# Queueing the expert rows of a gather behind the sums on VectorE, and lending it one weight buffer

## The chip, the core and the metric

The kernel is one program on one core of a Trainium2 chip. The metric is device time in microseconds. Three timed runs of the kernel before gave 3833.3, 3834.04 and 3835.98 us; the median is 3834.04 us. One further execution was taken by the profiler, and all rows below are of that one.

## The reference, cut to what matters

The program computes two transformer blocks over 512 tokens of width 1024. All work of this change lies in the last step of the second block, a feed-forward layer that looks up experts:

```python
def peer_ffn(h, peer_w_q, peer_keys_1, peer_keys_2, peer_u, peer_v):
    ht = h.reshape(T, D)                       # T = 512 tokens, D = 1024
    ...                                        # scores, top 16 of 128 x 128 pairs, 8 heads
    experts = (...).reshape(T, 128)            # 128 expert numbers of 16384 per token
    gates = softmax(sc).reshape(T, 128)
    u = peer_u[experts]                        # 128 rows of 1024 per token
    act = gelu(einsum('cd,ced->ce', hc, u))
    return einsum('ce,ced->cd', gates * act, peer_v[experts])

h = layer_norm(ALPHA * h + peer_ffn(h, ...), ln2_g, ln2_b)
```

## The kernel before, in words

The 512 tokens are split. For the last 384 of them the layer is computed densely: TensorE multiplies them by all of `peer_u`, the gelu of the products is multiplied by a matrix of gates that is zero outside the chosen experts, and the result is multiplied by all of `peer_v`. For the first 128 tokens the chosen rows are gathered from HBM, one expert of each of the 128 tokens at a time.

**The dense part.** Weights come as chunks of 128x1024 f32 (512 KB). `Stream` holds four raw buffers. `load` (L148) issues the chunk's DMA from SyncE's queue as soon as a raw buffer is free. `cut` splits a chunk into a high and a low half: ScalarE casts the high half (L155), VectorE subtracts it to get the low half (L157), and then the raw buffer is free again. There are three pairs of split buffers, so that the cut of a chunk waits until the product three before it has read its pair. A product is 24 matmuls (L281, L282, L283; the third reads the low half) of 128x384 into one PSUM bank. There are 128 "u" products (`ups`, first matrix) and 128 "v" products (second matrix, 16 groups `c` of 8). 31 u products are made ahead of the last loop; in the loop each v product from the ninth on is followed by one u product until all 128 are made, and the last 23 v products stand alone. Behind each v product the code lists, in this order: `weigh` (L2005 on VectorE multiplies a gelu by its gates; L287 on ScalarE and L288 on VectorE split it), `settle` of the v product before (L2032 on VectorE adds its PSUM bank to the sum), and `rows`, which is the gather.

**The gather.** It is a generator. `fetch(n)` (L1953) is an indirect DMA on GpSimd's queue that brings 512 KB, one row of 1024 f32 for each of 128 tokens, into one of three row buffers. Rows 0 to 127 come from the first matrix, and L1966 on VectorE multiplies each by the token's state and sums it up to one number; rows 128 to 255 come from the second, and L1968 on VectorE adds each, times its gate, to an accumulator. Before row n is used, the fetch of row n + 2 is issued; it must wait until row n - 1 has been used, whose buffer it takes. After row 255 there is a layer norm of the first 128 tokens (L1974 to L1985) and its store.

`rows(products)` paces the gather in the order of the code: 256 rows over `work` = 128 + 128 - 31 - 8 = 217 products. That is the order in which the code lists the instructions. The order on the engines is made by a planner, which keeps time estimates of its own: an instruction that it takes to be ready is put on its engine ahead of instructions listed earlier. Each engine then runs its own list strictly in order.

Of the kernel before, what the change touches and what calls it, by code (L numbers as in the profile page):

```python
# [10 lines left out]
OP = mybir.AluOpType  # L11
AX = mybir.AxisListType

D = 1024
# [13 lines left out]
ALPHA = 2.0**0.25  # L28
# [7 lines left out]
class Buf:  # L36
    def __init__(self, arena, off, n, ap):
        self.arena, self.off, self.n, self.ap = arena, off, n, ap
# [78 lines left out]
class Stream:  # L117
# [6 lines left out]
    def __init__(self, k, order=None, nraw=4, nsplit=3):  # L124
        self.k, self.order, self.nraw, self.nsplit = k, order, nraw, nsplit
        self.chunks = {}
        self.free = [k.F(1024, top=True) for _ in range(nraw)]
        self.hl = [(k.R(1024, top=True), k.R(1024, top=True)) for _ in range(nsplit)]
        self.rest = k.nc.vector
        self.asked = []  # L130
        self.seen = {}
        self.held = False
        self.loaded = self.split = self.cuts = self.used = 0
        self.whole = None

    def add(self, key, aps):
        c = self.chunks.setdefault(key, [])
# [3 lines left out]
    def load(self, i):  # L141
# [6 lines left out]
        self.k.nc.sync.dma_start(c[1].ap, c[0])  # L148
        return True

    def cut(self, i):
        key, n = self.order[i]
        c = self.chunks[key][n]
        hi, lo = self.hl[self.cuts % self.nsplit]
        self.k.nc.scalar.copy(hi.ap, c[1].ap)  # L155
        eng = self.rest[i % len(self.rest)] if isinstance(self.rest, list) else self.rest
        eng.tensor_tensor(lo.ap, c[1].ap, hi.ap.bitcast(F32), op=OP.subtract)  # L157
        self.free.append(c[1])
        c[1] = hi.ap, lo.ap
        self.cuts += 1  # L160

# [60 lines left out]
class K:  # L222
# [1508 lines left out]
    def peer(self):  # L1731

        nc = self.nc
# [20 lines left out]
        sel0 = self.F(384, top=True)  # L1754
# [65 lines left out]
        def up(j):  # L1820
            for _ in ups(j):
                pass
# [5 lines left out]
        for n in range(16):  # L1828
            if n in first:
                ps = first[n]  # L1830
            else:
                hi, lo = self.ws.get("wq")
                ps = self.bank()
# [54 lines left out]
        for t in (1, 2, 3):  # L1888
            sv3 = st.v(4, 128)
            nxt = None  # L1890
            for g in range(16):
                c = slice(g * 8, g * 8 + 8)
# [12 lines left out]
                if fused:  # L1905
                    for r in range(8):
                        q = slice(g * 8 + r, g * 8 + r + 1)
                        nc.vector.tensor_scalar(e2[:, r * 128 : r * 128 + 128], iota.ap, sv3[:, 1, q], sv3[:, 2, q],  # L1908
                                                op0=OP.is_equal, op1=OP.mult)
                else:  # L1910
                    w = e2.rearrange("p (a b) -> p a b", a=8)
                    nc.gpsimd.tensor_tensor(w, w, sv3[:, 2, c, None].to_broadcast([128, 8, 128]), op=OP.mult)
                stage = stages[g // 2 % len(stages)]
                for half in range(2):
                    ps = self.bank()
                    for q in range(4):
                        r = half * 4 + q
                        w = slice(r * 128, (r + 1) * 128)
# [12 lines left out]
            st.free()  # L1931
            st = nxt
        row.free()
        while ahead < sum(UPS):
            up(ahead)
            ahead += 1
            yield 3.9
# [6 lines left out]
        def gather():  # L1944

            s0 = sel0.v(3, 128)
            ids, act0 = self.F(128), self.F(128)
            acc0 = self.F(D)
            rows = [self.F(D) for _ in range(3)]

            def fetch(n):
                if n < 256:
                    nc.gpsimd.indirect_dma_start(out=rows[n % 3].ap, out_offset=None, in_=self.a["u" if n < 128 else "vv"],  # L1953
                                                 in_offset=bass.IndirectOffsetOnAxis(ap=ids.ap[:, n % 128 : n % 128 + 1].bitcast(U32), axis=0))

            nc.vector.scalar_tensor_tensor(act0.ap, s0[:, 0], 128.0, s0[:, 1], op0=OP.mult, op1=OP.add)
            nc.vector.tensor_copy(ids.ap.bitcast(U32), act0.ap)
            nc.vector.tensor_scalar(acc0.ap, ht.ap, ALPHA, None, op0=OP.mult)
            for n in range(2):
                fetch(n)  # L1960
            yield
            for n in range(256):
                r = rows[n % 3].ap
                fetch(n + 2)
                if n < 128:
                    nc.vector.scalar_tensor_tensor(r, r, 1.0, ht.ap, op0=OP.mult, op1=OP.mult, accum_out=act0.ap[:, n : n + 1])  # L1966
                else:
                    nc.vector.scalar_tensor_tensor(acc0.ap, r, act0.ap[:, n - 128 : n - 127], acc0.ap, op0=OP.mult, op1=OP.add)  # L1968
                if n == 127:
                    nc.scalar.activation(act0.ap, act0.ap, AF.Gelu_apprx_tanh)  # L1970
                    nc.vector.tensor_mul(act0.ap, act0.ap, s0[:, 2])
                yield
            for j in range(2):
                nc.gpsimd.dma_start(rows[j].ap, self.a["ln2"][:, j * D : (j + 1) * D])  # L1974
            w, scr = self.F(8), rows[2].ap
            W = w.ap
            nc.vector.tensor_reduce(W[:, 0:1], acc0.ap, axis=AX.X, op=OP.add)
            nc.vector.tensor_scalar(W[:, 0:1], W[:, 0:1], 1.0 / D, None, op0=OP.mult)
            nc.vector.tensor_scalar(acc0.ap, acc0.ap, W[:, 0:1], None, op0=OP.subtract)
            nc.scalar.activation(scr, acc0.ap, AF.Square, accum_out=W[:, 1:2])  # L1980
            nc.scalar.activation(W[:, 2:3], W[:, 1:2], AF.Sqrt, bias=self.eps6.ap[:, 1:2], scale=1.0 / D)
            nc.vector.reciprocal(W[:, 3:4], W[:, 2:3])
            nc.vector.scalar_tensor_tensor(scr, acc0.ap, W[:, 3:4], rows[0].ap, op0=OP.mult, op1=OP.mult)
            nc.vector.tensor_add(scr, scr, rows[1].ap)
            nc.sync.dma_start(self.out0, scr)  # L1985
            for x in rows + [w, acc0, sel0, ids, act0]:
                x.free()


# [23 lines left out]
        for g in range(2):  # L2013
            ps = self.bank()
# [8 lines left out]
        for k in range(KT):  # L2023
            nc.gpsimd.tensor_tensor(av[:, k].rearrange("p (t n) -> p t n", t=3), hh[:, 1:, k].bitcast(F32),
                                    hl[:, 1:, k].bitcast(F32), op=OP.add)
        gat = gather()
        down = []

        def settle(c, d, seg, ps):
            c0, c1 = seg  # L2030
            x = av[:, d, c0:c1]
            nc.vector.scalar_tensor_tensor(x, x, ALPHA if c == 0 else 1.0, ps.ap[:, : c1 - c0], op0=OP.mult, op1=OP.add)  # L2032
            ps.free()
            if c == 15:
                t = tot[seg]
                if d == 1:
                    nc.vector.tensor_add(t.ap, av[:, 0, c0:c1], x)
                elif 1 < d < 7:
                    nc.vector.tensor_add(t.ap, t.ap, x)

        self.ws.rest = nc.vector
        ws = {}
        work = 128 + 128 - ahead - 8
        paced = [0, 0]

        def rows(products):

            paced[0] += products
            while paced[1] < 256 * paced[0] // work:
                next(gat, None)  # L2050
                paced[1] += 1


# [11 lines left out]
        for c in range(16):  # L2065
            cur = [ws.pop(c * 8 + j) for j in range(8)]
            for seg in last if c == 15 else [(0, N)]:
                c0, c1 = seg
                if c == 15:
                    tot[seg] = self.F(c1 - c0)  # L2070
                for d in range(8):
                    hi, lo = self.ws.get("v_b" if c0 else "v")
                    ps = self.bank()
                    for j in range(8):
                        self.mm3(ps.ap[:, : c1 - c0], hi[:, j * 128 : (j + 1) * 128], lo[:, j * 128 : (j + 1) * 128],
                                 *[w[:, c0:c1] for w in cur[j]], j == 0, j == 7)
                    self.ws.done()
                    n = 1
                    if c and ahead < 128:
                        n = 2  # L2080
                        up(ahead)
                        ahead += 1
                        if ahead == 128:
                            gelu(*late.pop())
                        yield 3.9
                    weigh(c * 8 + 8 + d)
                    down.append((c, d, seg, ps))
                    if len(down) > 1:
                        settle(*down.pop(0))
                    rows(n)  # L2090
                    if not c0 and d in (1, 3, 5):
                        gload(c + 2, d // 2)
                    self.tick()
                    yield 3.9
                if c == 15:
                    settle(*down.pop(0))
                    if seg != last[-1]:
                        self.later(self.last_norm(av, seg, tot[seg]))
# [438 lines left out]
```

## Time and profile before

| what | value |
|---|---|
| median of three timed runs | 3834.04 us |
| profiled execution | 3846.21 us, span of its trace 3844.5 us |
| TensorE (PE) busy | 3598.5 us, 94% of the span |
| VectorE (DVE) busy | 2461.9 us, 64% |
| ScalarE (ACT) busy | 1455.4 us, 38% |
| GpSimd (POOL) busy | 711.4 us, 19% |
| mean granted clock of TensorE | 0.971 of full speed |

PE are matmuls, PEld their weight loads. The loop with the gather is the last part of the span, from about 2782 us; the page's row of 40 slices shows DMA engines busy at 8 and 9 tenths in slices 29 to 37 and at 2 to 4 tenths in most others. A group of the view by lines reads: line, engine, operation, result <- operands, shapes, count | busy us, mean ns of one | idle us of that engine just before them and what ended it. DVE durations overlap their neighbours' a little at the ends.

### The profile page before, as it was taken

To read this page: it belongs to the slowest core of one execution; us is meant where nothing else is said; L and a number is where in the kernel's file an instruction comes from. 1 tells how busy PE (TensorE), PEld (TensorE's weight loads), DVE (VectorE), ACT (ScalarE), POOL (GpSimd) and SP (SyncE) were. 2 spreads that over 40 slices of the span, in tenths; PEclk is the share of its full clock that TensorE was granted. 3 is DMA by queue.
4 is the path that set the end of the run, shared out by engine and by line. 5 is a ranking of instruction groups with operands and counts; after the bars stand their busy time and mean duration, and the time that the engine had idled before them with its cause. 6 is when DMAs were issued, how large, how long until landed. Compare 5 with 4: busy or idle time off the path is not lost. (4 is left out here: it accounts for less than half of the span.)

```text
span 3844.5 us, 51080 instructions
## 1 busy us (share of the span) xinstructions
PE 3598.5 (94%) x20063; PEld 3168.7 (82%) x20063; DVE 2461.9 (64%) x4157; ACT 1455.4 (38%) x2351; POOL 711.4 (19%) x511
## 2 busy tenths in 40 slices
PE   7999899999999999998999898888889999999997
PEld 4766588888888888887888867878789999889997
DVE  6543675343466555657544657898988777777754
ACT  5323444222244333335323546425633333332332
POOL 1111100000000000000000110665534444444200
PEclk9999999999999999998999998999999999999998
DMA  5355432212122212122322312324788888888732
GB/s 204 118 197 187 151 127 85 65 62 65 62 95 89 73 63 86 58 75 72 115 95 97 129 60 95 102 85 143 211 309 313 305 304 308 291 302 298 269 126 72
DMA packets 199597, 573.38 MB, mean 149 GB/s; under 512 B 17051, under 2 KB 67227, under 8 KB 199356
## 3 DMA queue, kind: packets, MB, share of 16 engines
q1 hardware_dynamic: 100224, 362.33, 28.7%
q0 software_dynamic: 42416, 156.57, 11.4%
q10 hardware_dynamic: 56716, 51.22, 4.0%
q8 instruction: 157, 2.57, 0.3%
q14 instruction: 84, 0.69, 0.0%
HBM read 539.64 MB, written 30.41 MB: 148 GB/s over the span
## 5 line engine op out<-in xcount | busy, mean ns | idle before, releaser
L155 ACT CAST ra<-fa 128x1024 fp32r<-128x1024 f32 x591 | 620.1, 1051 | 1591.6 <-PE P L282 655.0
L157 DVE TENSOR_TENSOR ra<-fa,ra 128x1024 fp32r<-128x1024 f32 x543 | 663.0, 1223 | 491.2 <-ACT ra L155 484.2
L282 PE MATMUL P<-ra 128*128 128x512 f32 (+1 forms) x1952 | 694.5, 357 | 2.9 <-DVE ra L288 2.7
L283 PE MATMUL P<-ra 128*128 128x512 f32 (+1 forms) x1872 | 675.3, 363 | 2.4 <-DVE ra L157 2.4
L281 PE MATMUL P<-ra 128*128 128x512 f32 (+1 forms) x1824 | 651.0, 364 | 21.1 <-ACT ra L287 17.4
L283 PE MATMUL bank<-ra 128*128 128x384 f32 (+2 forms) x1648 | 564.4, 343 | 63.1 <-DVE ra L157 41.8
L281 PE MATMUL bank<-ra 128*128 128x384 f32 (+2 forms) x1648 | 561.7, 342 | 13.0 <-ACT ra L287 11.4
L282 PE MATMUL bank<-ra 128*128 128x384 f32 (+2 forms) x1648 | 560.0, 340 | 8.3 <-DVE ra L288 8.3
L281 PE MATMUL P<-mR,ra 128*128 128x512 f32 (+1 forms) x1344 | 464.7, 349 | 12.8 <-ACT mR L287 8.6
L283 PE MATMUL P<-mR,ra 128*128 128x512 f32 (+1 forms) x1344 | 459.2, 343 | 0.3 <-DVE ra L157 0.3
L282 PE MATMUL P<-mR,ra 128*128 128x512 f32 (+1 forms) x1216 | 424.3, 350 | 1.0 <-DVE mR L288 1.0
L282 PEld LDWEIGHTS P<-ra 128*128 128x128 f32 x1952 | 375.4, 192 | 56.1 <-DVE ra L288 3.7
L281 PEld LDWEIGHTS P<-ra 128*128 128x128 f32 x1824 | 346.7, 192 | 78.7 <-ACT ra L287 19.5
L283 PEld LDWEIGHTS P<-ra 128*128 128x128 f32 x1872 | 357.9, 191 | 57.7 <-DVE ra L157 3.7
L283 PEld LDWEIGHTS bank<-ra 128*128 128x128 f32 x1648 | 317.7, 193 | 79.9 <-DVE ra L157 53.2
L281 PEld LDWEIGHTS bank<-ra 128*128 128x128 f32 x1648 | 317.8, 193 | 17.8 <-ACT ra L287 12.0
L282 PEld LDWEIGHTS bank<-ra 128*128 128x128 f32 x1648 | 317.9, 193 | 12.5 <-DVE ra L288 9.3
L876 DVE SCALAR_TENSOR_TENSOR fa<-P,fa 128x512 f32<-128x512 f32 (+1 forms) x256 | 164.1, 641 | 221.8 <-PE P L283 221.4
L281 PEld LDWEIGHTS P<-mR,ra 128*128 128x128 f32 x1344 | 257.5, 193 | 52.7 <-ACT mR L287 10.0
L283 PEld LDWEIGHTS P<-mR,ra 128*128 128x128 f32 x1344 | 256.7, 192 | 31.1 <-DVE ra L157 1.1
L282 PEld LDWEIGHTS P<-mR,ra 128*128 128x128 f32 x1216 | 232.0, 191 | 32.5 <-issue 2.2
L1968 DVE SCALAR_TENSOR_TENSOR fa<-fa 128x1024 f32<-128x1024 f32 x128 | 164.0, 1281 | 87.4 <-DMA fa<-in_vv,fa 86.9
(418 smaller groups left out, 5395.2 us busy)
## 6 DMA issues: line engine op xcount, KB each, us to landing
fa<-in_w SPq DMA_DIRECT2D x144, 512.0 KB, 3.7
fa<-in_ud SPq DMA_DIRECT2D x128, 512.0 KB, 4.8
fa<-in_vd SPq DMA_DIRECT2D x128, 512.0 KB, 5.7
fa<-in_ada SPq DMA_DIRECT2D x96, 512.0 KB, 4.9
fa<-in_od_in SPq DMA_DIRECT2D x66, 512.0 KB, 3.7
gd<-fa ACTq DMA_DIRECT2D x24, 1024.0 KB, 5.3
trio<-gd ACTq DMA_DIRECT2D x48, 512.0 KB, 9.0
fa<-in_w_q SPq DMA_DIRECT2D x22, 512.0 KB, 3.8
```

The costliest lines, as they stand in the source:

```text
L155: self.k.nc.scalar.copy(hi.ap, c[1].ap)
L157: eng.tensor_tensor(lo.ap, c[1].ap, hi.ap.bitcast(F32), op=OP.subtract)
L281: mm(ps, wh, xh, start=start, stop=False)
L282: mm(ps, wh, xl, start=False, stop=False)
L283: mm(ps, wl, xh, start=False, stop=stop)
L876: self.nc.vector.scalar_tensor_tensor(x, ps, g[:, n, kind : kind + 1], x, op0=OP.mult, op1=OP.add)
L1968: nc.vector.scalar_tensor_tensor(acc0.ap, r, act0.ap[:, n - 128 : n - 127], acc0.ap, op0=OP.mult, op1=OP.add)
```

## The change

Each step of the gather is listed with an order edge: its VectorE instructions stand on VectorE's list behind the last `settle` that the code has listed (`issue_after`; it is an order, not a wait for a semaphore). The gather gets a fourth row buffer, and the fetch of row n + 3 is issued before row n is used. The fourth buffer is one of `Stream`'s four raw buffers: the first chunk that is cut after the page stage gives its buffer to the gather (`lend`) instead of back to the stream, which has three from then on.

```diff
@@ class Stream @@
+    def lend(self, f):
+
+        self.lent = f
...
     def cut(self, i):
...
-        self.free.append(c[1])
+        if self.lent:
+            self.lent(c[1])
+            self.lent = None
+        else:
+            self.free.append(c[1])
@@ def peer @@
         row.free()
+        lent = []
+        self.ws.lend(lent.append)
         while ahead < sum(UPS):
             up(ahead)
...
-            rows = [self.F(D) for _ in range(3)]
+            own = [self.F(D) for _ in range(3)]
+            rows = own + lent
 
             def fetch(n):
                 if n < 256:
-                    nc.gpsimd.indirect_dma_start(out=rows[n % 3].ap, ...
+                    nc.gpsimd.indirect_dma_start(out=rows[n % 4].ap, ...
...
-            for n in range(2):
+            for n in range(3):
                 fetch(n)
             yield
             for n in range(256):
-                r = rows[n % 3].ap
-                fetch(n + 2)
+                r = rows[n % 4].ap
+                fetch(n + 3)
...
-            for x in rows + [w, acc0, sel0, ids, act0]:
+            for x in own + [w, acc0, sel0, ids, act0]:
                 x.free()
@@ def settle @@
-            nc.vector.scalar_tensor_tensor(x, x, ALPHA if c == 0 else 1.0, ps.ap[:, : c1 - c0], op0=OP.mult, op1=OP.add)
+            i = nc.vector.scalar_tensor_tensor(x, x, ALPHA if c == 0 else 1.0, ps.ap[:, : c1 - c0], op0=OP.mult, op1=OP.add)
+            settled[:] = [getattr(i, "ins", i)]
...
+        settled = []
@@ def rows @@
             while paced[1] < 256 * paced[0] // work:
-                next(gat, None)
+
+                with self.tc.issue_after(settled[0]) if settled else nullcontext():
+                    next(gat, None)
                 paced[1] += 1
```

## Rows read from the trace of the kernel before

**Rows 1.** Busy time by stretch: stretch, length, engines busy (count), PE clock, DMA share, GB/s
```profile
2782.00:2860.00 78.00, 64.20 (x353) 62.87 (x352) 59.80 (x103) 27.06 (x44) 28.55 (x25) 0.89 0.85 301
2860.00:3620.00 760.00, 717.36 (x4015) 704.36 (x4014) 598.10 (x772) 240.73 (x332) 314.92 (x240) 0.98 0.87 304
3620.00:3817.00 197.00, 197.00 (x1139) 197.00 (x1138) 102.40 (x133) 66.62 (x88) 0.55 (x1) 1.00 0.37 121
```
**Rows 2.** What PE waited for from 2860 to 3620: us in total, times, longest
```profile
PE bank L283 <- DVE ra L157: 41.4, 29, 4.5
```
**Rows 3.** What DVE waited for from 2860 to 3620
```profile
DVE fa L1968 <- DMA fa<-in_vv,fa: 86.9, 55, 4.9
DVE fa L1966 <- DMA fa<-in_u,fa: 74.2, 50, 4.1
```
**Rows 4.** DVE in order of time: start, us, line, operation, idle before and its end
```profile
3342.94 1.29 DVE L1968 SCALAR_TENSOR_TENSOR fa<-fa 128x1024 f32<-128x1024 f32 x1 [1.34 <-DMA fa<-in_vv,fa]
...
3348.77 2.61 DVE L1968 SCALAR_TENSOR_TENSOR fa<-fa 128x1024 f32<-128x1024 f32 x2 [2.95 <-DMA fa<-in_vv,fa]
3351.29 1.22 DVE L157 TENSOR_TENSOR ra<-fa,ra 128x1024 fp32r<-128x1024 f32 x1
```
**Rows 5.** ACT in order of time, the same stretch
```profile
3345.46 1.05 ACT L155 CAST ra<-fa 128x1024 fp32r<-128x1024 f32 x1 [2.32 <-PE bank L282]
```
**Rows 6.** PE in order of time, the same stretch
```profile
3352.57 0.44 PE L283 MATMUL bank<-ra 128*128 128x384 f32 x1 [2.23 <-DVE ra L157]
```
**Rows 7.** The gather's fetches, line L1953, up to 3204 us (durations in ns)
```profile
L1953 POOL DMA_INDIRECT fa<-in_u,fa x127: 932/1016/1878, 2786.5 to 3199.4; - x127
...
DMA to landing us min/median/max: 4.2/6.8/12.6
```
**Rows 8.** The same from 3206 to 3620 us
```profile
L1953 POOL DMA_INDIRECT fa<-in_vv,fa x128: 936/1295/3286, 3206.5 to 3615.1; - x128
...
DMA to landing us min/median/max: 4.2/7.0/11.2
```
**Rows 9.** POOL in order of time: a fetch behind the row that frees its buffer
```profile
3344.49 0.94 POOL L1953 DMA_INDIRECT fa<-in_vv,fa  x1 [2.09 <-DVE fa L1968]
```
**Rows 10.** DVE by lines from 2860 to 3620
```profile
L157 DVE TENSOR_TENSOR ra<-fa,ra 128x1024 fp32r<-128x1024 f32 x168 | 204.2, 1218 | 0.0
L1968 DVE SCALAR_TENSOR_TENSOR fa<-fa 128x1024 f32<-128x1024 f32 x127 | 162.7, 1281 | 87.3 <-DMA fa<-in_vv,fa 86.9
L1966 DVE SCALAR_TENSOR_TENSOR fa<-fa 128x1024 f32<-128x1024 f32 x114 | 139.1, 1221 | 74.6 <-DMA fa<-in_u,fa 74.2
L2005 DVE TENSOR_TENSOR cols<-cols,trio 128x384 f32<-128x384 f32 x84 | 46.2, 550 | 0.0
L2032 DVE SCALAR_TENSOR_TENSOR fa<-fa,bank 128x384 f32<-128x384 f32 x84 | 45.9, 546 | 0.0
L288 DVE TENSOR_TENSOR cols<-cols 128x384 fp32r<-128x384 f32 x45 | 24.8, 550 | 0.0
L288 DVE TENSOR_TENSOR ra<-cols,ra 128x384 fp32r<-128x384 f32 x35 | 17.8, 550 | 0.0
```
**Rows 11.** The weights' loads, line L148, from 2786 to 3620 us
```profile
L148 SPq DMA_DIRECT2D fa<-in_vd x91: 327/328/328, 2788.4 to 3616.5; - x91
...
who waited for it (us, times):
  ACT ra L155: 3.9, 1
...
DMA to landing us min/median/max: 3.6/5.9/13.2
```
**Rows 12.** What SyncE's queue waited for from 2860 to 3620
```profile
SPq L148 <- DVE ra L157: 691.9, 168, 8.8
```
**Rows 13.** DVE in order of time: the last two sums of products
```profile
3813.49 0.55 DVE L2032 SCALAR_TENSOR_TENSOR fa<-fa,bank 128x384 f32<-128x384 f32 x1 [3.01 <-PE bank L283]
...
3817.65 0.56 DVE L2032 SCALAR_TENSOR_TENSOR fa<-fa,bank 128x384 f32<-128x384 f32 x1 [3.02 <-PE bank L283]
```
**Rows 14.** DVE in order of time: the gather's last rows and the end of its layer norm
```profile
3619.72 2.60 DVE L1968 SCALAR_TENSOR_TENSOR fa<-fa 128x1024 f32<-128x1024 f32 x2
...
3630.72 1.22 DVE L1984 TENSOR_TENSOR fa<-fa 128x1024 f32<-128x1024 f32 x1
```
**Rows 15.** What PE waited for from 2780 to 2860
```profile
PE bank L281 <- ACT ra L287: 6.0, 1, 6.0
PE bank L282 <- DVE ra L288: 4.8, 1, 4.8
PE bank L283 <- DVE ra L157: 2.8, 1, 2.8
```

More of the change, by code (lines that the diff above doesn't have):

```diff
@@ L1 @@
 import math
+from contextlib import nullcontext
 import numpy as np
@@ L133, in __init__ @@
         self.loaded = self.split = self.cuts = self.used = 0
-        self.whole = None
+        self.whole = self.lent = None
     def add(self, key, aps):
@@ L1948, in gather @@
             acc0 = self.F(D)
-            rows = [self.F(D) for _ in range(3)]
+            own = [self.F(D) for _ in range(3)]
+            rows = own + lent
             def fetch(n):
                 if n < 256:
-                    nc.gpsimd.indirect_dma_start(out=rows[n % 3].ap, out_offset=None, in_=self.a["u" if n < 128 else "vv"],
+                    nc.gpsimd.indirect_dma_start(out=rows[n % 4].ap, out_offset=None, in_=self.a["u" if n < 128 else "vv"],
                                                  in_offset=bass.IndirectOffsetOnAxis(ap=ids.ap[:, n % 128 : n % 128 + 1].bitcast(U32), axis=0))
```

## The prediction, written before the change was run

> **What bounds the kernel now.** I read the busy times by stretch first. From 3620 us on, when the gather is over, TensorE never stops: 1139 matmuls in 197.0 us at full granted clock, 173.0 ns each [rows 1]. The last two sums, one product apart, start 4.16 us apart [rows 13]: 24 matmuls of 173.3 ns. That is the cadence of this loop when nothing is late. From 2860 to 3620 us, beside the gather, 4015 matmuls take 760 us [rows 1]; at the cadence they would take 4015 x 0.1733 = 695.8 us. So 64 us are lost beside the gather, and this is all that a change to the gather can win here.
>
> The view of waits says who takes them. TensorE waits 41.4 us in 29 waits, practically all of its idle time there, for the low half of a weight chunk, which VectorE cuts [rows 2]. The other 23 us go with the clock: it was granted at 0.98 on the mean in this stretch against 1.00 behind it [rows 1]. Mean 0.98 of the levels 1.2 and 2.4 GHz is 4% of the time at the low one, 30 us, half of which is lost; the rest is the restart after each wait.
>
> VectorE is busy 598 of the 760 us [rows 1], so it isn't full. Its idle time is 161 us, all of it spent at the head of a gather row whose DMA had not landed, in 105 of 241 rows [rows 3, 10]. Three rows in order of time show how this reaches TensorE. ScalarE's half of a cut starts at 3345.46 [rows 5] and ends 1.05 us later. VectorE's half could follow; but two gather rows stand ahead of it, the first of them waits 2.95 us for its DMA, and the cut starts at 3351.29 [rows 4], 4.8 us after its input. TensorE waits 2.23 us for it [rows 6].
>
> **Why the rows are late.** With three row buffers, a fetch starts when the row three before has been used: the row at 3342.94 ends at 3344.23 and its buffer's fetch starts at 3344.49, 0.26 us later [rows 4, 9]. It lands 6.8 to 7.0 us after its start on the median, 12.6 at most [rows 7, 8]. So a buffer turns round in 0.3 + 6.9 + 1.3 (the row itself [rows 10]) = 8.5 us, and three buffers give at best a row per 2.8 us. The rows were planned faster than the DMAs could bring them: 241 rows for 84 sums of products [rows 10], 2.87 per v product. The code lists 2 x 256 / 217 = 2.36 per v product with its u product.
>
> **The change, part by part.**
>
> *The edge.* A v and a u product last 8.32 us at the cadence. With the edge no more than 2.36 rows on the mean stand behind each sum, so a row is wanted every 3.53 us.
>
> *The fourth buffer.* Four buffers of 8.5 us give a row per 2.1 us at best, well ahead of 3.53. But rows now come in bursts of 2 or 3 behind each sum, back to back. Row n is fetched when row n - 4 ends. At 2.36 on the mean, 36% of the bursts have three rows. Most rows have two bursts of lead, over 14 us, more than any landing. The tight ones are: the second row of a burst of two behind a burst of three (fetched behind the first row of the burst before; 8.3 us), and the third row of a burst of three behind a burst of two (8.32 + 1.2 = 9.5 us). Each occurs in about 36% of 97 pairs. A landing is 0.3 + 6.9 = 7.2 us after the buffer is free on the median, and from 4.5 to 12.9. I estimate that a third of the first kind and a sixth of the second come late, by 1.2 us: 97 x 0.36 x 0.5 x 1.2 = 21 us of VectorE waiting instead of 161. In this trace 161 us of it cost TensorE 64 us, 0.40 each; so 8 us stay lost. Bounds: 0 if no row is late enough to matter (a cut has slack, below), 32 us if half of the waiting stays.
>
> The Trainium skill, "DMA: Bandwidth & Descriptors", section "Anatomy of one DMA", gives a DMA from GpSimd's queue as about 2.0 us plus its bytes at 436 GB/s: an estimate of 3.2 us for 512 KB. The trace shows 6.8 to 7.0 beside the weights' loads, and by 3.2 us three buffers would never have been late, which they were 105 times; the measurement decides. By the page, the 8 us would be 0 and the time 8 us less.
>
> *VectorE's load.* Per pair: two cuts of 1.22, one sum, one `weigh` and one split of 0.55 each, and 2.36 rows of 1.25 us are 7.04 us nominal [rows 10]. The lines of the view add up to 650 us of which 598 are distinct (ends overlap [rows 1, 10]), so 6.5 of 8.32 us, 78%. The worst queue ahead of a cut is a sum and three rows, 0.5 + 3 x 1.2 = 4.1 us from the end of a product; the cut's input is ready 1.2 us after the same moment, so the low half is ready 5.3 us after it and is wanted two products later, at 8.3. 3 us of slack: this hides the burst, and a row that is late by less.
>
> In the last 23 v products, which stand alone, the gather still has 256 - 2 x 97 x 256 / 217 - 9 = 18 rows, over 15 products. There VectorE has 1.22 + 3 x 0.55 + 1.18 x 1.28 = 4.38 nominal, 4.03 distinct, per 4.16 us. This phase runs without loss today because the gather is over [rows 1]. Cost 0 at 4.03, 15 x (4.38 - 4.16) = 3 us at the nominal price; I take 3, since waits for ScalarE come on top.
>
> *The gather's end.* Its layer norm takes 11 to 12 us behind the last row [rows 14]. It is listed behind product 218 of 225, so with 29 us of products still to come, and the other tokens' norm of 27 us behind these [rows 1]: hidden. If the rows fell 15 us behind, it would start to compete with the last norm.
>
> *Three raw buffers.* Each load is issued at the end of a cut, 168 times of 168 [rows 12]. The cut of product i waits for the end of product i - 3; it then takes 1.05 on ScalarE, a delay d until VectorE comes to it, and 1.22. The load behind it, now for product i + 3, lands 5.9 us later (13.2 at most [rows 11]); it is wanted 3 products = 12.48 us after the cut could start. So 8.2 + d against 12.48 us: d may be 4.3 us. In the forecast d is 0 to 3 us. If a chunk is late, its own cut may still slip by 6 - d us before TensorE waits. Four buffers never ran dry (one wait of 3.9 us, at the start [rows 11]). I take 0; the other end is the last rival.
>
> *The start.* From 2782 to 2860 us TensorE loses some 22 us, half of it waiting for the first weighted columns [rows 1, 15], which the change doesn't touch; 2.8 us wait for a cut [rows 15]. I take 0, between 3 us lost (a third fetch ahead of the first loads) and 5 won.
>
> **The sum.** 64 - 8 - 3 = 53 us. The profiled execution took 3846.2 us, 1.7 over its span; it becomes 3793. The median of the timed runs lies 12.2 us under the profiled one, so 3834 - 53 = 3781 us.
>
> **The rivals.**
>
> *Rows still late.* Two or three fetches now start within 4 us of each other, and GpSimd writes them one by one, 1.0 to 1.3 us each and up to 3.3 [rows 7, 8]. If the landing of a burst's last fetches grows by 2 us, the 8.3 us kind is late as a rule and the 9.5 us kind half the time: 97 x 0.36 x (1.5 + 0.8) = 80 us of VectorE waiting, 32 us of TensorE's. Gain 64 - 32 - 3 = 29: 3805 us. For it: the spread from 4.2 to 12.6 us. Against it: the pace falls from 2.87 to 2.36 rows per pair, and with it the load on the DMA engines of 0.87. A rule of the Trainium skill would make it so: by "SBUF — State Buffer", section "Who interferes with whom", a VectorE instruction with two SBUF inputs keeps a GpSimd instruction that reads SBUF waiting, and a burst is several such instructions end to end. The long fetch of 3.3 us would fit that; the medians near 1.0 and 1.3 us, beside a VectorE that was busy 79% of the stretch, speak against a regular cost.
>
> *It doesn't do what it says.* The edge keeps rows from running ahead, but whether a cut stands behind them is still the planner's choice. If VectorE waits for rows as long as now, or idles at the head of a sum for the product's end and is as late with cuts, the 64 us stay: 3834 us. Against it: 8.5 us of turn-round against 4 x 3.53.
>
> *Three raw buffers starve TensorE.* This decides for slower, in one place: the loop load, cast, cut, load. A late chunk costs TensorE, per pair, (2.3 + d + landing) - 12.48 - (6 - d) = landing + 2d - 16.2 us. With the 4.8 us of delay seen at 3351 in every v product's cut and landings of 7.5 us, it is 0.9 us x 97 = 87 us lost against 64 won: 3857 us. It starts to cost at landings of 6.6 us with that d, at 10.2 with d = 3, and to outweigh the gain 0.7 us above either. Landings reach 13.2 us [rows 11], but the median is 5.9, and d of 4.8 came from a DMA wait that the change shortens.
>
> **How the numbers follow.** Forecast 3781 us, chance 0.62, with its own range of 3764 (all 64 us and some of the start) to 3797 (16 us more lost). Rows still late, 3797 to 3822: 0.20. Nothing won, about 3834: 0.08. Starved, from 3842 up: 0.10. Two tenths lie outside 3762 to 3812, nearly all above. A difference under 0.2%, 7.7 us, can't be told from none here. Faster takes the first two, 0.82.
>
> **What would show it.** Right: in the loop, VectorE's waits for rows fall from 161 to about 20 us and TensorE's for L157 from 41 to under 10; the granted clock is 0.99 or 1.00; sums come 8.3 us apart beside u products; the last row is used some 30 us before the last product's end, not 200. Wrong: VectorE's wait for rows stays above 80 us; ScalarE's casts wait for the weights' DMA; TensorE waits in the last 23 products; or the end waits for the gather's norm.

## The result, and the profile after

The changed kernel took 3779.07 us (median of four runs, 3772.22 to 3780.1) against 3835.01 for the kernel before (its three runs and a fourth of 3843.63): a ratio of 0.9842 (95% interval 0.983 to 0.9855). Forecast were 3781 us. Its profiled execution took 3780.1 us, its trace spans 3778.4.

Busy time by stretch, the changed kernel (stretch, length, then PE, PEld, DVE, ACT, POOL busy with counts, PE clock, DMA share, GB/s):

```profile
2782.00:2860.00 78.00, 67.19 (x378) 65.62 (x377) 60.19 (x104) 29.16 (x45) 31.28 (x25) 0.91 0.85 289
2860.00:3620.00 760.00, 757.61 (x4372) 757.29 (x4371) 600.74 (x784) 261.39 (x360) 310.28 (x216) 1.00 0.85 300
3620.00:3751.00 131.00, 131.00 (x757) 131.00 (x756) 100.04 (x120) 42.93 (x57) 37.31 (x26) 1.00 0.63 214
```

Beside the gather, the same 760 us now hold 4372 matmuls instead of 4015 [rows 1]. At 173.3 ns each they account for 757.7 us, so 2 us are lost where 64 were. The granted clock is 1.00. The last 131 us, with the v products that stand alone and the end of the gather among them, lose nothing. What TensorE and VectorE wait for from 2860 to 3620 us, the changed kernel (settle is L2044 now, the gather's rows L1978 and L1980, a chunk's cast and low half L160 and L162):

```profile
PE bank L292 <- DVE ra L162: 2.4, 1, 2.4
```
```profile
DVE fa L2044 <- PE bank L292: 93.2, 82, 1.6
DVE ra L162 <- ACT ra L160: 57.6, 54, 1.4
DVE fa L1978 <- DMA fa<-in_u,fa: 7.4, 4, 3.2
DVE fa L1980 <- DMA fa<-in_vv,fa: 0.4, 1, 0.4
```

TensorE's 29 waits for a low half [rows 2] have become one. VectorE's idle time has changed its owner: before it stood at rows that had not landed [rows 3]; now it stands at the head of a sum whose product TensorE hasn't finished, or of a low half whose cast ScalarE hasn't made. VectorE now waits for TensorE, 82 times of the 92 sums. VectorE's list in order of time:

```profile
3302.28 0.56 DVE L2044 SCALAR_TENSOR_TENSOR fa<-fa,bank 128x384 f32<-128x384 f32 x1 [1.31 <-PE bank L292]
3302.75 1.28 DVE L1980 SCALAR_TENSOR_TENSOR fa<-fa 128x1024 f32<-128x1024 f32 x1
3303.95 1.22 DVE L162 TENSOR_TENSOR ra<-fa,ra 128x1024 fp32r<-128x1024 f32 x1
3305.09 1.28 DVE L1980 SCALAR_TENSOR_TENSOR fa<-fa 128x1024 f32<-128x1024 f32 x1
3307.35 1.23 DVE L162 TENSOR_TENSOR ra<-fa,ra 128x1024 fp32r<-128x1024 f32 x1 [0.99 <-ACT ra L160]
3308.49 0.55 DVE L2017 TENSOR_TENSOR cols<-cols,trio 128x384 f32<-128x384 f32 x1
3308.96 0.55 DVE L297 TENSOR_TENSOR cols<-cols 128x384 fp32r<-128x384 f32 x1
3310.60 0.56 DVE L2044 SCALAR_TENSOR_TENSOR fa<-fa,bank 128x384 f32<-128x384 f32 x1 [1.09 <-PE bank L292]
```

Two sums start 8.32 us apart: two products at the cadence. Here, with rows of the second matrix, they are not in a block behind the sum; the planner has set a low half between them, 0.8 us after its cast (ScalarE's cast of this chunk starts at 3302.11 and takes 1.05 us). With rows of the first matrix they are: from 2860 to 3620 us three of them stand end to end behind a sum 16 times and two 29 times. One of the 16 (the lines of the accumulator's read left out):

```profile
2944.52 0.56 DVE L2044 SCALAR_TENSOR_TENSOR fa<-fa,bank 128x384 f32<-128x384 f32 x1 [1.09 <-PE bank L292]
2944.99 1.22 DVE L1978 SCALAR_TENSOR_TENSOR fa<-fa 128x1024 f32<-128x1024 f32 x1
...
2946.14 1.22 DVE L1978 SCALAR_TENSOR_TENSOR fa<-fa 128x1024 f32<-128x1024 f32 x1
...
2947.28 1.22 DVE L1978 SCALAR_TENSOR_TENSOR fa<-fa 128x1024 f32<-128x1024 f32 x1
...
2948.43 2.39 DVE L162 TENSOR_TENSOR ra<-fa,ra 128x1024 fp32r<-128x1024 f32 x2
```

The gather's DMAs land no sooner than before:

```profile
DMA to landing us min/median/max: 4.8/7.7/13.5
```

But they are issued so much earlier that a row lies landed for 4.4 us on the median before VectorE takes it, instead of 0.15 us before (each fetch of the stretch matched with its row in the two traces).

### The profile page after: what moved, and what is told of

The parts are those of the page before. It is cut to its first block, busy times and chain, and to the rows that moved or that the text cites. A ratio compares the mean times of both kernels' runs of the same rounds, so it can differ in the third digit from the quotient of the medians.

```text
span 3778.4 us, 51080 instructions
## 1 busy us (share of the span) xinstructions
PE 3578.4 (95%) x20063; PEld 3161.0 (84%) x20063; DVE 2463.2 (65%) x4157; ACT 1452.7 (38%) x2349; POOL 746.2 (20%) x511
## 5 line engine op out<-in xcount | busy, mean ns | idle before, releaser
L160 ACT CAST ra<-fa 128x1024 fp32r<-128x1024 f32 x591 | 620.2, 1051 | 1534.2 <-PE P L291 653.9
L162 DVE TENSOR_TENSOR ra<-fa,ra 128x1024 fp32r<-128x1024 f32 x543 | 663.2, 1224 | 508.2 <-ACT ra L160 501.3
L292 PE MATMUL bank<-ra 128*128 128x384 f32 (+2 forms) x1648 | 555.1, 338 | 21.0 <-POOL ra L162 21.0
L290 PE MATMUL bank<-ra 128*128 128x384 f32 (+2 forms) x1648 | 556.4, 339 | 13.3 <-ACT ra L296 12.0
L291 PE MATMUL bank<-ra 128*128 128x384 f32 (+2 forms) x1648 | 555.1, 337 | 7.1 <-DVE ra L297 7.1
L292 PEld LDWEIGHTS bank<-ra 128*128 128x128 f32 x1648 | 313.9, 191 | 26.8 <-POOL ra L162 23.4
L290 PEld LDWEIGHTS bank<-ra 128*128 128x128 f32 x1648 | 314.0, 191 | 17.9 <-ACT ra L296 12.6
L291 PEld LDWEIGHTS bank<-ra 128*128 128x128 f32 x1648 | 314.2, 191 | 11.3 <-DVE ra L297 8.1
L1965 POOL DMA_INDIRECT fa<-in_vv,fa x128 | 189.3, 1479 | 265.9 <-DVE fa L1980 251.6
```

The lines of the kernel that those rows point to most:

```text
L290: mm(ps, wh, xh, start=start, stop=False)
L291: mm(ps, wh, xl, start=False, stop=False)
L292: mm(ps, wl, xh, start=False, stop=stop)
L1965: nc.gpsimd.indirect_dma_start(out=rows[n % 4].ap, out_offset=None, in_=self.a["u" if n < 128 else "vv"], in_offset=bass.IndirectOffsetOnA ...
```

## Experiments

All were timed against the kernel before. The third column is 760 us less 0.1733 us for each matmul in the stretch from 2860 to 3620 us, from each run's own busy times, as for the 64 us of before [rows 1]; the fourth is what VectorE waited there for rows' DMAs; then rows per v product with its u product, counted on VectorE.

| kernel | ratio (95% interval) | TensorE loses, us | VectorE waits for rows, us | rows per pair |
|---|---|---|---|---|
| before (three buffers) | 1 | 64 | 161 | 241 / 84 = 2.87 |
| the change | 0.9842 (0.983 to 0.9855) | 2 | 8 | 216 / 92 = 2.35 |
| edge alone (three) | 0.9833 (0.982 to 0.9847) | 5 | 73 | 217 / 91 = 2.38 |
| edge alone, again | 0.9851 (0.9836 to 0.9866) | 0 | 64 | 218 / 92 = 2.37 |
| buffer alone (four) | 0.9856 (0.9841 to 0.9871) | 3 | 42 | 195 / 66 = 2.95 |
| edge, three, pace 2.75 | 0.9968 (0.9958 to 0.9978) | 44 | 153 | 239 / 86 = 2.78 |
| edge, three, pace 3.0 | 0.9984 (0.9972 to 0.9996) | 58 | 152 | 242 / 85 = 2.85 |
| edge, four, pace 3.0 | 0.9858 (0.9842 to 0.9873) | 4 | 30 | 192 / 65 = 2.95 |
| no fetches | 0.9825 (0.9811 to 0.9838) | 0 | 0 | 223 / 65 = 3.4 |

(For the buffer alone, for four buffers at pace 3.0 and for the kernel without fetches, the rows per pair are of 2860 to 3400 us, as their gathers end within the longer stretch. In the last of them rows are no DMAs, but VectorE's instructions.)

**The edge alone.** The change without `lend`, three row buffers, the fetch two rows ahead.

```diff
-        self.ws.lend(lent.append)
...
-            rows = own + lent
+            rows = own
...
-            for n in range(3):
+            for n in range(2):
                 fetch(n)
...
-                r = rows[n % 4].ap
-                fetch(n + 3)
+                r = rows[n % 3].ap
+                fetch(n + 2)
```

> The order edge alone: three row buffers, the fetch two rows ahead, four raw weight buffers. My theory: edge and buffer are both needed. A row is wanted every 3.53 us and three buffers of 8.5 us can bring one per 2.8, so on the mean they keep up; but the lead of a row is 3 x 3.53 - 1.25 = 9.3 us (less where rows stand together) against landings of 7.2 us on the median and up to 12.9, so a good part of the rows is late: VectorE waits 50 to 100 us for rows instead of 161, TensorE's loss is 20 to 40 us of 64, the time 0.989 to 0.995 of before. Rival A, the pace is the whole gain: VectorE waits under 20 us, the time is that of the full change, 0.984 to 0.986. Rival B, the buffer is the whole gain: VectorE waits 130 us or more and the time is within 0.3% of before.

It came out as fast as the full change. VectorE waits 73 us for rows, as my theory had it; TensorE loses 5 us, not 20 to 40. Its waits from 2860 to 3620 us, TensorE's and VectorE's (L1977 and L1979 are the rows here):

```profile
PE bank L292 <- DVE ra L162: 3.7, 4, 1.7
```
```profile
DVE fa L2043 <- PE bank L292: 58.1, 59, 1.6
DVE fa L1977 <- DMA fa<-in_u,fa: 57.6, 38, 5.2
DVE ra L162 <- ACT ra L160: 25.7, 28, 1.3
DVE fa L1979 <- DMA fa<-in_vv,fa: 14.9, 15, 2.2
```

In 53 waits, one of 5.2 us, a late row holds VectorE up, and TensorE hardly notices. So "late rows cost TensorE 0.40 us each microsecond" is false, and so is "edge and buffer are both needed".

**The fourth buffer alone.** The change without `issue_after`.

```diff
-                with self.tc.issue_after(settled[0]) if settled else nullcontext():
-                    next(gat, None)
+                next(gat, None)
```

> The fourth row buffer lent by the weights alone, without the order edge. My theory: both are needed. Without the edge the planner lets the gather run as fast as it thinks that four buffers can bring rows, 8.5 / 4 = 2.1 us per row or 3.9 rows per 8.32 us; with these VectorE has 3.7 + 3.9 x 1.2 = 8.4 us of work per 8.32 us, so it is full, and any row that lands late delays a cut. The gather ends near 3400 us, VectorE still waits 60 us or more for rows, TensorE loses 25 to 60 us, the time is 0.988 to 0.999 of before. Rival A, the pace is the whole gain: VectorE waits as long as before and the time is within 0.3% of before. Rival B, the buffer is the whole gain: VectorE waits under 20 us, 0.984 to 0.986.

As fast again, though rows now come at 2.95 per pair, more than before. My theory fails a second time: VectorE waits 42 us and TensorE loses 3. Either half of the change does nearly the whole work, and neither rival, which give it to one half only, is right. What TensorE waits for and VectorE's waits for rows from 2860 to 3620 us, then the busy time by stretch:

```profile
PE bank L292 <- DVE ra L162: 1.5, 2, 0.8
```
```profile
DVE fa L1978 <- DMA fa<-in_u,fa: 26.7, 24, 3.4
DVE fa L1980 <- DMA fa<-in_vv,fa: 15.2, 15, 2.9
```
```profile
2782.00:2860.00 78.00, 61.58 (x338) 60.02 (x337) 59.09 (x104) 25.71 (x41) 34.74 (x29) 0.87 0.88 310
2860.00:3400.00 540.00, 538.22 (x3101) 537.12 (x3101) 476.87 (x636) 187.62 (x260) 259.63 (x194) 1.00 0.93 339
```

What this kernel lacks against the full change stands at the loop's start: from 2782 to 2860 us it holds 338 matmuls instead of 378, some 6 us.

**No fetches.** The kernel before with the indirect DMAs of rows 2 to 255 left out.

```diff
-                if n < 256:
+                if n < 2:
...
-                r = rows[n % 3].ap
+                r = rows[n % 2].ap
-                    nc.vector.scalar_tensor_tensor(r, r, 1.0, ht.ap, ...
+                    nc.vector.scalar_tensor_tensor(rows[2].ap, r, 1.0, ht.ap, ...
```

> The kernel before, with the indirect DMAs of rows 2 to 255 left out: VectorE still runs all 256 row instructions, on two rows fetched once, so the gather's sums are not computed. It is the floor of what late rows cost. My theory: everything lost beside the gather comes from rows that land late. VectorE never waits for a row, TensorE runs at the cadence of 173.3 ns per matmul in the loop, and the time is 0.982 to 0.986 of before, that of the full change. The rival, that the amount of VectorE work beside the products costs part of it (the planner then packs rows even denser at the front), leaves TensorE waits for low halves of 10 us or more and 0.987 to 0.995.

Busy time by stretch, this kernel:

```profile
2860.00:3400.00 540.00, 540.00 (x3117) 540.00 (x3116) 510.47 (x660) 187.95 (x260) 0.00 (x0) 1.00 0.44 151
```

VectorE is busy 510 of 540 us, 95%, fuller than in any other run, and TensorE loses nothing. So it was the wait for the rows' DMAs, and not the amount of VectorE's work, that held TensorE in the kernel before. Leaving out the fetches also halves the traffic, but traffic alone isn't the cause: with the fourth buffer alone it was 339 GB/s in this stretch, in the kernel before 307, and the loss was gone. The rival with 10 us or more of waits is out.

**Two raw buffers for the weights.** The change with two buffers lent, the second left idle.

```diff
+        self.lend_n = 2
...
             self.lent(c[1])
-            self.lent = None
+            self.lend_n -= 1
+            if not self.lend_n:
+                self.lent = None
...
-            rows = own + lent
+            rows = own + lent[:1]
```

> The full change with two raw weight buffers lent instead of one: the gather still uses four row buffers (the second lent one lies idle), the weights keep two. It prices the loop of load, cast, cut and load: 5.9 to 6.5 us of landing, 1.05, a delay of about 1, and 1.22 are 9.7 us, against 8.32 us in which two raw buffers must turn round. My theory of that loop says 1.4 us or more too long per two products, over 225 products some 150 us of lateness, less what shorter landings give back when the loads thin out: slower than before, 1.005 to 1.03, with ScalarE's casts waiting for the weights' DMA. The rival, that the weights have so much slack that raw buffers don't matter here, says the same time as the full change, 0.984 to 0.986.

0.9828 (0.9813 to 0.9844): the time of the full change, as the rival said. What ScalarE waits for from 2860 to 3620 us (L161 is the cast here):

```profile
ACT ra L161 <- PE bank L294: 330.9, 124, 5.2
ACT ra L161 <- DMA fa<-in_vd: 50.1, 15, 6.5
ACT ra L161 <- DMA fa<-in_ud: 30.9, 10, 7.1
```

25 casts do wait for their load, 81 us in all, and TensorE waits for none of them in this stretch. My loop named the right place and a wrong price. What takes the lateness up was not tried by itself; by the prediction's own count a cut isn't wanted until two products later.

**A theory of rates.** The runs so far say that waits count only above some amount. VectorE's list is fixed when the kernel is built. If behind each sum the list holds more rows than the chip brings in the time of two products, the list as a whole falls behind, every cut with it, and nothing can make it up; if it holds fewer, a late row takes from idle time. In the kernel before: 760 us / 241 rows = 3.15 us per row, and 2.87 x 3.15 = 9.05 us per pair, against 8.32. That the product of the two is the time per pair is no evidence by itself; what can be tested is whether the price per row stays the same when the list asks for another pace. Three runs did this. The first two raise the code's pace, once in the kernel with the edge alone (three buffers), once in the full change (four):

```diff
-        work = 128 + 128 - ahead - 8
+        work = 170
```

> The edge with three row buffers, as in the run with the edge alone, but the code's pace raised from 256 rows per 217 products to 256 per 170: 3.0 rows per v and u product instead of 2.36. My new theory, a coupling of rates: VectorE's list is fixed, so the products can go no faster than the listed rows behind each sum times the time that the chip takes per row. In the kernel before that is 241 rows for 84 sums in 760 us, 2.87 x 3.15 us = 9.05 us per pair of products instead of 8.32; a wait that is shorter than this costs nothing, since it is made up. Then this run must lose again: 2.8 to 3.0 listed rows x 3.15 us = 8.8 to 9.4 us per pair, until the gather is over after some 85 pairs: 45 to 80 us lost against the run with the edge alone, 0.993 to 1.002 of before. The rival, that the edge helps by where it puts rows and cuts in the list and not by the pace, says the time of the edge alone, 0.982 to 0.985.

> The same raised pace of 3.0 rows per pair with the edge, but with the fourth row buffer as in the full change. By the coupling of rates the chip's time per row falls from 3.15 to some 2.4 us, so 3.0 rows take 7.1 us of 8.32: no loss, the time of the full change, 0.982 to 0.987 of before, although VectorE waits for rows in many places. The rival, that VectorE's load decides (3.7 + 3.0 x 1.2 = 7.3 us per pair), says some 10 to 30 us lost beside this, 0.987 to 0.993.

With three buffers the gain is gone, edge or no edge: 0.9984. VectorE by lines from 2860 to 3620 us, three buffers at this pace:

```profile
L1979 DVE SCALAR_TENSOR_TENSOR fa<-fa 128x1024 f32<-128x1024 f32 x127 | 162.8, 1282 | 79.5 <-DMA fa<-in_vv,fa 78.8
L1977 DVE SCALAR_TENSOR_TENSOR fa<-fa 128x1024 f32<-128x1024 f32 x115 | 140.2, 1221 | 73.6 <-DMA fa<-in_u,fa 73.5
L2043 DVE SCALAR_TENSOR_TENSOR fa<-fa,bank 128x384 f32<-128x384 f32 x85 | 46.5, 547 | 0.0
```

242 rows in 760 us are 3.14 us per row, the price of the kernel before [rows 10], and no sum waits for TensorE any more. With four buffers the same pace loses 4 us; its lines from 2860 to 3400 us:

```profile
L1978 DVE SCALAR_TENSOR_TENSOR fa<-fa 128x1024 f32<-128x1024 f32 x112 | 135.7, 1219 | 13.9 <-DMA fa<-in_u,fa 13.8
L1980 DVE SCALAR_TENSOR_TENSOR fa<-fa 128x1024 f32<-128x1024 f32 x80 | 102.4, 1280 | 11.0 <-DMA fa<-in_vv,fa 10.6
L2044 DVE SCALAR_TENSOR_TENSOR fa<-fa,bank 128x384 f32<-128x384 f32 x65 | 35.8, 550 | 6.1 <-PE bank L292 6.1
```

540 us / 192 rows: four buffers can bring a row per 2.81 us or better (the buffer alone, 195 rows: 2.77). The rival of the order in the list is out (the edge is there in both), and so, by a loss of 4 us instead of 10 to 30, is that of VectorE's load, though the ratio's interval reaches up to its 0.987.

A pace between was the third test, `work = 186` with the edge and three buffers:

> The edge with three row buffers at a pace between the two: 256 rows per 186 products, 2.75 per pair (2.36 lost nothing, 3.0 lost 58 us). By the coupling of rates the pair takes the longer of 8.32 us and 2.75 x 3.14 = 8.64 us: 0.32 us more, over some 85 pairs 27 us, 0.989 to 0.993 of before. A threshold of another kind, at which all of the loss sets in at once, says 0.997 or more; one above 2.75 says 0.985 or less.

0.9968, outside the 0.989 to 0.993 that I gave and just short of the step at 0.997. Its trace from 2860 to 3620 us:

```profile
L1979 DVE SCALAR_TENSOR_TENSOR fa<-fa 128x1024 f32<-128x1024 f32 x124 | 159.0, 1282 | 79.1 <-DMA fa<-in_vv,fa 78.6
L1977 DVE SCALAR_TENSOR_TENSOR fa<-fa 128x1024 f32<-128x1024 f32 x115 | 139.7, 1222 | 76.0 <-DMA fa<-in_u,fa 74.4 <-issue 1.5
L2043 DVE SCALAR_TENSOR_TENSOR fa<-fa,bank 128x384 f32<-128x384 f32 x86 | 47.1, 548 | 0.0
```

There are 239 rows and 86 sums in 760 us: 3.18 us per row, and 2.78 rows per pair. The product of the two, 8.84 us per pair, is 760 / 86 again, so it can't confirm the loss of 44 us. What the run adds is a third price: 3.15, 3.14 and 3.18 at three paces, against 3.50 where the list asks for no more. The three paces lie close together, 2.78 to 2.87. The forecast missed because the loss is a difference of two nearly equal times: 0.03 rows and 0.04 us above what I had put in are 0.2 us per pair, 17 us over 86 pairs. The loss was 44 us at 2.78 and 5 or less at 2.38. Nothing was run between these two, so a step at some pace between them is not ruled out; the interval reaches the 0.997 that I gave for it.

**Bursts.** The full change, `rows` called behind every second v product with the rows of two.

```diff
-                    rows(n)
+                    owed[0] += n
+                    if d % 2:
+                        rows(owed[0])
+                        owed[0] = 0
```

> The full change, but the gather is called behind every second v product with the rows of two: bursts of 4 or 5 rows per 16.6 us instead of 2 or 3 per 8.3, at the same mean pace. The prediction's step that rows in bursts come late, each microsecond of VectorE's waiting costing TensorE 0.40: the fifth row of a burst takes a buffer freed within the same burst, 5 us late, 48 x 0.7 x 5 = 170 us of VectorE waiting and 68 us lost, back near the time before. The coupling of rates says: the mean pace is unchanged and far below what four buffers bring, so lateness inside a burst is made up within 16 us; VectorE waits more, some 50 to 150 us, TensorE under 10 us, 0.983 to 0.988 of before.

0.9838 (0.9824 to 0.9851); from 2860 to 3620 us VectorE waits 17 us for rows, less than the 50 to 150 us of the theory of rates, and TensorE loses 2. VectorE's order of time shows that the bursts did come. With rows of the first matrix four of them stand end to end behind a sum 23 times, and then low halves ahead of the fifth, the one that was to be 5 us late (accumulator's reads left out):

```profile
2916.93 1.22 DVE L1978 SCALAR_TENSOR_TENSOR fa<-fa 128x1024 f32<-128x1024 f32 x1
...
2918.08 2.35 DVE L162 TENSOR_TENSOR ra<-fa,ra 128x1024 fp32r<-128x1024 f32 x2
2920.35 1.22 DVE L1978 SCALAR_TENSOR_TENSOR fa<-fa 128x1024 f32<-128x1024 f32 x1
```

Its buffer came free 5.6 us before it started, and its fetch landed in 5.0 us. Rows of the second matrix are drawn apart by low halves sooner:

```profile
3314.15 1.28 DVE L1980 SCALAR_TENSOR_TENSOR fa<-fa 128x1024 f32<-128x1024 f32 x1
3315.35 1.22 DVE L162 TENSOR_TENSOR ra<-fa,ra 128x1024 fp32r<-128x1024 f32 x1
3316.49 2.60 DVE L1980 SCALAR_TENSOR_TENSOR fa<-fa 128x1024 f32<-128x1024 f32 x2
3319.00 1.22 DVE L162 TENSOR_TENSOR ra<-fa,ra 128x1024 fp32r<-128x1024 f32 x1
```

**Repeats, and a try at the rest.** The changed kernel again, and the edge alone again:

> The changed kernel once more, beside these on the same chip: 0.983 to 0.9855 of before, by every theory.

> The edge alone once more (three row buffers, four raw weight buffers), beside the next two on one chip: 0.982 to 0.985 of before. If the fourth row buffer added something that the edge alone doesn't give, the full change's 0.9842 and 0.9835 would lie clear below this; by the coupling of rates the two are the same, and the buffer need not be lent.

0.9835 (0.9821 to 0.985) and 0.9851 (0.9836 to 0.9866). The two kernels can't be told apart.

What is left near the loop is the moment before it: from 2782 to 2860 us the changed kernel has 10.8 us without a matmul and a granted clock of 0.91 over the other 67, some 17 us lost. Two runs kept more products for it (`UPS[3]` = 5 and 7, with the edge alone):

> The edge alone with 5 instead of 3 products of the first matrix kept for the moment between the page stage and the loop (33 made ahead instead of 31). There TensorE loses some 18 us in every version, waiting for the gates' way through HBM and back to speed after it. Two products more are 8.3 us of work that move out of the loop into that wait: 5 to 8 us less than the edge alone, 0.9805 to 0.983 of before. The rival, that what waits there is not TensorE's work but the start of the weights' and gates' DMAs and VectorE's first columns, which the two products only push back, says no change within 0.1%.

> The same with 7 products kept (35 made ahead): 10 to 16 us less than the edge alone if TensorE's wait is what is filled, 0.978 to 0.982 of before; no more than with 5 if the wait is about 9 us long and the rest is the lower clock behind it; worse, if the gelus, for which there are 32 buffers, must wait for the first columns to be used.

0.984 (0.9827 to 0.9854) and 0.9835 (0.9822 to 0.9849): no change beyond the intervals, so the forecasts of 5 to 8 us and of 10 to 16 us less were wrong. With 7, TensorE is busier there, but the first sum comes at 2833 us instead of 2815 to 2817. VectorE from 2860 to 3620 us, 7 products kept:

```profile
DVE fa L1977 <- DMA fa<-in_u,fa: 62.0, 40, 4.1
DVE fa L2043 <- PE bank L292: 41.9, 36, 2.9
DVE fa L1979 <- DMA fa<-in_vv,fa: 40.8, 30, 4.7
```

That is 103 us of waiting for rows, at a loss of 5 us. Where the moved products' time went was not followed further. No run beat the change beyond its interval.

## Why the prediction was right, step by step

*What bounds the kernel: right.* Nearly all of the gain is in the stretch of the gather: 62 us of the 66 between the two spans. Low halves late behind rows that had not landed were the carrier, and without fetches nothing is lost.

*Why a late row costs TensorE: wrong.* The step took 161 us of waiting to cost 64, "0.40 each", and used this as a price. The runs show no such price: waits of 8, 42, 64, 73 and 103 us cost 0 to 5 us, waits of 152, 153 and 161 us cost 58, 44 and 64. In the three that lose, rows take practically all of VectorE's idle time (161 of 162 us, 153 of 155, 152 of 156) and no sum waits for TensorE; with the edge alone they take 73 of 157, and sums wait 58 us for TensorE. What counts is whether the list asks for rows faster than three buffers bring them. The prediction says that it does, but its own rates don't: 8.5 / 3 = 2.8 us per row would just have kept up with 8.32 / 2.87 = 2.90. It left two parts out of the turn-round. Matched fetch by fetch with its row in the trace of the kernel before, a landing takes 7.2 us on the mean (6.9 is the median), and a landed row waits 0.8 us more for its turn on VectorE. With 0.35 us from the free buffer to the fetch and 1.25 for the row that is 9.5 us, or 3.2 per row, and this is over 2.90.

*The edge: right in its number* (2.36 rows per pair forecast, 2.35 found), *and more than a part*: it alone removes the loss, with a row wanted every 3.50 us against a price of 3.15. It does so through the pace, since with the pace raised the same edge gains only 0.2% (0.9984); a lower pace without the edge was not run.

*The fourth buffer: mis-sized.* 21 us of VectorE's waiting were forecast and 8 us came, in 5 waits; 8 us of loss were forecast and 2 came. Both tight kinds of rows occurred, 33 times each. Their buffers came free 8.2 and 9.4 us ahead on the median in the first matrix's half, where 8.3 and 9.5 were forecast, and 9.4 and 10.7 us in the second's. What failed is that they were given the landing of all rows: theirs took 6.3 and 7.4 us on the median, the other rows' 8.0, and VectorE waited for 3 of the first kind, 1 of the second and 1 other row, where 12 and 6 were forecast. Why they land sooner was not tried. The Trainium skill, "Perfetto Trace Analysis", section "Optimization Strategy", says that a gap which keeps coming back on the engine that should be full can mean too few buffers. The trace agrees, as the fourth buffer alone shows (0.9856); the edge alone shows that asking for less does as well (0.9833 and 0.9851).

*The last 23 v products: mis-sized.* 3 us were forecast; the stretch from 3620 us lost nothing.

*The gather's end and three raw buffers: right at 0.* The last row is used at 3718, 33 us before the last sum at 3751.6. The layer norm behind it took 10.5 us (9.6 in the kernel before [rows 14], where the prediction read 11 to 12). Even two raw buffers cost nothing.

*The start: inside its bounds.* It was taken at 0 and won 4 us: 378 matmuls from 2782 to 2860 us instead of 353 [rows 1].

*The sum.* Profile against profile the gain was 66 us, not 53: 9 us of the difference are the two residues (6 of the 8 us and the 3), 4 are the start. The median moved by 56 us (62 in the repeat), as the profiled execution of the kernel before was one of its longer ones (3846.2, when the runs of it in these studies go from 3827.6 to 3846.7) and that of the changed kernel is 1.0 us over its median, not 12.2. Two errors, of 13 and 11 us, took each other away in 3781: that the forecast is within 2 us is luck; that most of the 64 us came back is not.

*The rivals.* Rows still late: the landings did grow, from 6.8 to 7.0 us to 7.7, and a fetch takes 1.68 us of GpSimd on the median instead of 1.0 to 1.3 [rows 7, 8]; a row wanted every 3.53 us left four buffers room for both. The longer fetch isn't the fourth buffer's doing: with the edge alone it takes 1.68 us too, with four buffers at pace 3.0 again 1.0 to 1.3. Nor does it follow VectorE's load, which is higher at that pace (473 of 540 us, against 427 in the changed kernel); its cause stays open. Starvation did not come, and the run with two raw buffers shows that its price was far too high. That the change doesn't do what it says is out.

## What to carry to other kernels

Where an engine runs a fixed list in order and some of its entries wait for DMAs, compare two rates first: entries listed per step of the main loop times the time per entry (a buffer's round trip, measured in the trace with the queueing in it, divided by the number of buffers), against the step. Below, late entries cost next to nothing, here up to 103 us of waiting in 760; above, the whole loop runs at the gather's pace. How sharp the line between is was not measured. Then either ask for fewer per step or add a buffer; one of the two was enough here, and the order edge costs no memory.

## What the runs showed of the hardware that was not expected

With four buffers the landing of a row got longer, not shorter: 7.7 us on the median (7.4 in the repeat, 7.8 at pace 3.0) against 6.8 to 7.0 [rows 7, 8], and 7.0 with the edge and three buffers at pace 3.0. The changed kernel moves 300 GB/s in the stretch, the one before 304 [rows 1]. The cause was not tried. A weight chunk's load, 5.9 us on the median beside the gather [rows 11], takes 3.6 us in the kernel without fetches. The weights' chunks, with 512 KB each per product of 4.16 us, run from two raw buffers without a loss of TensorE's.
